# A two-level Winograd matmul with bias and tanh: output stores issued by ScalarE, the first columns of B loaded in wider runs, the first bias load placed later

## The chip, the cores and the metric

The kernel runs on one core of a Trainium2 chip. The core has five engines, each with its own queue of instructions: TensorE (PE in the profile; its weight loads are PEld), VectorE (DVE), ScalarE (ACT), GpSimd (POOL) and SyncE (SP). In this kernel POOL and SP issue all the DMAs. The metric is the device time of one execution in microseconds (us); the median of several runs is compared.

## The reference

```python
m, k, n = 4096, 4096, 4096        # a: [m, k], b: [k, n], bias: [n], all float32
def reference(a, b, bias):
    return np.tanh(np.matmul(a, b) + bias)
```

## The kernel before

**The arithmetic.** A and B are cast to fp16 while they are loaded, products accumulate in fp32 in PSUM (8 banks of 128 x 512), and the output is float32. The output's columns are worked in four groups of 1024 (`c` = 0 to 3); in a group B is cut in four blocks, b11 and b12 (upper half of K, left and right 512 columns), b21 and b22 (lower half of K). The rows of A go in 16 pairs of 128-row tiles, with a11, a12, a21 and a22 likewise. A pair needs seven products in place of eight, by Winograd's scheme: the sums of A's blocks are `s1` to `s4`, those of B's are `t1` to `t4`, and the products are P1 to P7. Many of these products are cut once more by the same scheme: `fine_right` (line 672) makes the sums of a block of B (`f1`, `f2`, `f3`, `f4`), `fine_left` (line 534) those of A (`y`, `z`, `v`), and the seven small products `p1` to `p7` have 256 columns each (`fine_product`, line 702, matmuls at line 709). Whole products have 512 columns (`product`, line 687, matmuls at line 694).

**The start.** The first eight row tiles of A (0 to 7) of the first column group are done without the scheme, straight from `land`ed tiles (lines 1318 to 1496, matmuls at line 1402), so that PE can begin as soon as a few tiles are there. A is loaded in its natural layout and turned: A's first four tiles, `first` (line 1319, four POOL DMAs of 256-byte pieces), by TensorE transposes (`turn_first`, line 1434), all others by VectorE transposes (lines 437 and 1365). PE's order is fixed: `turn_first(0)`, `turn_first(1)`, `row(0)`, `turn_first(2)`, `row(1)`, `turn_first(3)`, `row(2)`, `row(3)` (k tile 0, both halves of 1024 columns), then k tile 1 of the four row tiles, then k tiles 2 and 3, one row tile and one half at a time. Then row tiles 4 to 7 are done over k tiles 0 to 7, and so on. Sums that must leave their bank for a while go to `spill` (ACT copies at line 405) and come back by VectorE (lines 1427 and 402). Where they come back for the last time the bias is added (`take_up` with `k0`), so the first bias is needed there.

**B's loads.** K is laid over the partitions in four quarters of 32 partitions. The usual load of a piece of B (`load_b`, line 604, with its DMAs at line 620) is four POOL DMAs, one for each quarter, each into 32 partitions. `raw_b` loads four k tiles of 512 columns into one buffer (destination runs of 512 fp16 elements). `both_columns` (line 1335) loads two k tiles of all 1024 columns into one buffer (runs of 1024), two buffers to a block. In group 0, the first four k tiles of b11 and b12 are loaded by neither: eight single DMAs (line 615), each one k tile of 512 columns over all 128 partitions; the other three blocks of b11 and b12 come by `raw_b`, and the lower half (b21, b22) by `both_columns`. A DMA of any of these forms moves 128 KB of fp16. A subtraction of blocks (`subtract`, line 632) is cut in as many instructions as the block with the most buffers has buffers.

**Buffers.** SBUF is handed out in 51 `places`; a buffer takes a place when the planner starts its first writer and gives it back when its last user is done. So a load can have to wait until the store of what lay in the place before has landed.

**The order of the work** is written out by a planner (`Plan`, lines 128 to 334). The kernel adds operations with an engine, a duration, reads and writes. `rank` gives each a due time, counted back from those that need it: a DMA's due time is earlier by its issue, by 2 us, by its bytes over a rate, and by 4 us more. With `soft`, an operation is due soon after what it needs. `schedule` then plays the run through: each engine in turn takes the ready operation with the earliest due time, if there is room for its buffers. The order in which they were taken is the order in each engine's queue on the chip, and each queue is worked strictly in order there. A DMA counts as one issue (0.34 us on SP, 0.55 on POOL for each part); its bytes flow in a model with two pipes, one for hardware DMAs (SP) and one for POOL's, which share the bandwidth, and `RING` limits how many may be under way in each (8 and 16).

**Stores.** All 256 output stores (128 x 512 float32, 256 KB) are issued by SP: 112 by `store` (line 413, DMA at line 416), 144 by `finish_in` (line 1045, DMA at line 1050). Each comes after a tanh on ACT that writes its source. SP also issues the bias loads (`load_bias`, line 775), the copies of A's turned tiles and sums to DRAM and back (`move`, line 485, DMA at line 493) and the partial sums `state` (lines 1186 and 1241).

**ACT's work** beside tanh is copies from PSUM to PSUM or SBUF (line 405). In a fine product (`Fine`, line 970) one of them stands between `p1` and `p2`: `p1` is made in bank `be`, ACT copies it to bank `al`, and `p2` is added there. `step` (line 1140) puts the third part of the product before (16 matmuls of 256 columns) between the two on PE.

Of the kernel before, what the change touches and what calls it, by code (L numbers as in the profile page):

```python
# [37 lines left out]
LATER = 6  # L38
PLAIN = (0, 0, 0, 0)
SMALL = 5  # L40
RING = (16, 8)
RISE = ((), (3, 3, 3, 3, 3, 3, 3, 3), (3, 4, 4, 4, 4, 4, 4, 4), (3, 4, 4, 4, 4, 4, 4, 4))
SECONDS = (0, 4, 5, 8)
STEEP = (
# [83 lines left out]
class Plan:  # L128
# [77 lines left out]
    def schedule(self):  # L206
        self.rank()
        places = Places(PLACES)
        queue = {cls: [] for cls in UNITS}
        for i, b in enumerate(self.bufs):  # L210
            if b.users:
                b.order = (b.due, i)
                insort(queue[b.cls], b.order)
        ready = {e: [] for e in ("PE", "DVE", "ACT", "POOL", "SP")}
        busy = dict.fromkeys(ready, 0.0)
        pipes = ([], [])
        clock = [0.0, 0]
        events = [(0.0, -1, 0)]
        for op in self.ops:
            op.left = len(op.preds)  # L220
            op.ready = 0.0
            if not op.left:
                insort(ready[op.eng], (op.due, op.n))
        done, small = 0, [0]
        under_way = dict.fromkeys(ready, 0)

        at_pe = [min(op.due for op in self.ops if op.eng == "PE")]

        def fits(op):
            want = [b for b in op.bufs if b.place is None]  # L230
            near = (at_pe[0] + (op.early or 1e9), 0)
            for b in want:
                until = min(b.order, near)
                e4, e2, e1 = (bisect_left(queue[cls], until) for cls in UNITS)
                w, h, q = places.room()
                same = sum(x.cls == b.cls for x in want) - 1
                q2 = max(0, (e1 - q + 1) // 2)
                if b.cls == "big":
                    e2 = min(e2, max(0, SMALL - small[0]))
                    ok = w > max(same, e4 + max(0, (e2 + q2 - h + 1) // 2))  # L240
                elif b.cls == "out":
                    ok = h + 2 * max(0, w - e4) > max(same, e2 + q2)
                else:
                    ok = q + 2 * max(0, h + 2 * max(0, w - e4) - e2) > max(same, e1)
                if not ok:
                    return False
            return not want or op.due <= at_pe[0] + min(op.reach, self.FAR if op.early else 1e9)

        def flow(now):

            live = [p for p in pipes if p]
            for p in live:
                p[0][0] -= (now - clock[0]) / len(live)
            clock[0] = now
            ended = False
            for p in live:
                while p and p[0][0] < 1e-6:
                    op = p.pop(0)[1]
                    op.done = now + 2.0
                    heapq.heappush(events, (op.done, op.n, 1))  # L260
                    ended = True
            return ended

        def next_flow(now):
            live = [p for p in pipes if p]
            if live:
                clock[1] += 1
                at = now + max(min(p[0][0] for p in live), 1e-6) * len(live)
                heapq.heappush(events, (at, clock[1], 3))

        while events:
            now = events[0][0]
            while events and events[0][0] <= now + 1e-9:
                _, n, kind = heapq.heappop(events)
                if kind == 3 and n == clock[1]:
                    flow(now)
                    next_flow(now)
                elif kind == 4:
                    op = self.ops[n]
                    flow(now)  # L280
                    pipes[op.hw].append([op.lag - 2.0, op])
                    next_flow(now)
                elif kind == 1:
                    op = self.ops[n]
                    done += 1
                    for b in op.bufs:
                        b.users -= 1
                        if not b.users:
                            places.give(b.place)
                            small[0] -= b.cls == "out"  # L290
                    if op.nbytes:
                        under_way[op.eng] -= op.parts
                        for s in op.succs:
                            s.left -= 1
                            if not s.left:
                                heapq.heappush(events, (now, s.n, 2))
                elif kind == 2:
                    op = self.ops[n]
                    insort(ready[op.eng], (op.due, op.n))
            for eng, waiting in ready.items():  # L300
                if busy[eng] > now + 1e-9:
                    continue
                for i, (_, n) in enumerate(waiting):
                    op = self.ops[n]
                    if op.nbytes and under_way[eng] + op.parts > RING[op.hw]:
                        break
                    if not fits(op):
                        continue
                    waiting.pop(i)
                    for b in op.bufs:  # L310
                        if b.place is None:
                            b.place = places.take(UNITS[b.cls])
                            small[0] += b.cls == "out"
                            queue[b.cls].remove(b.order)
                    op.start = now
                    if eng == "PE":
                        at_pe[0] = op.due
                    end = now + op.dur
                    busy[eng] = end
                    heapq.heappush(events, (end, -1, 0))  # L320
                    if op.nbytes:
                        under_way[eng] += op.parts
                        heapq.heappush(events, (end, n, 4))
                        break
                    op.done = end + op.lag
                    heapq.heappush(events, (op.done, n, 1))
                    for s in op.succs:
                        s.ready = max(s.ready, end if s.eng == eng else op.done)
                        s.left -= 1
                        if not s.left:  # L330
                            heapq.heappush(events, (s.ready, s.n, 2))
                    break
        assert done == len(self.ops), (done, len(self.ops))
        return sorted(self.ops, key=lambda op: (op.start, op.n))
# [3 lines left out]
def kernel(  # L338
# [73 lines left out]

    def store(o, row, col, n):
        add(
            "SP", 0.34,
            lambda: nc.sync.dma_start(out=out[ds(row * P, P), ds(col, n)], in_=o[ALL]),
            (o,), (), nbytes=P * n * 4, soft=1.0,
        )

# [181 lines left out]
    def block(name):  # L601
        return Block([new(name, [P, TB, NB], atoms=2 * TB)])

    def load_b(buf, c, k0, nt, j=None, t0=0, early=0.0):

        dx, dt = (1, QP) if k0 >= TB else (TB, 1)
        n, first = (2 * NB, c * NCW) if j is None else (NB, c * NCW + j * NB)
        k1 = k0 - k0 % TB
        off = b.offset + (k1 * QP + (k0 - k1) * dt) * N + first
        one = nt == 1  # L610

        def emit():
            if one:
                src = bass.AP(tensor=b.tensor, offset=off, ap=[[KQ * N, 4], [dx * N, QP], [1, n]])
                nc.gpsimd.dma_start(out=buf[ALL, t0], in_=src)
                return
            for q in Q_ORDER:
                src = bass.AP(tensor=b.tensor, offset=off + q * KQ * N, ap=[[dx * N, QP], [dt * N, nt], [1, n]])
                dst = buf[ds(q * QP, QP)]
                nc.gpsimd.dma_start(out=dst.rearrange("p t j n -> p t (j n)") if j is None else dst, in_=src)  # L620

        add(
            "POOL", 0.55 * (1 if one else 4), emit, (),
            ((buf, (2 * t0, 2 * t0 + 1)) if one else buf,),
            nbytes=nt * P * n * 4, hw=False, early=early, rate=325e3 if j is not None else 362e3,
        )

# [144 lines left out]

    def load_bias(c):
        k = {}
        k["b1"] = new("bias", [P, 2, NB], fp32, atoms=2)
        src = bias[ds(c * NCW, NCW)]
# [3 lines left out]
                out=k["b1"][ALL].rearrange("P a b -> P (a b)"),  # L782
                in_=bass.AP(tensor=src.tensor, offset=src.offset, ap=[[0, P], *src.ap]),
            ),
            (), (k["b1"],), nbytes=P * NCW * 4,
        )
        return k

# [256 lines left out]
    def finish_in(tl, s, row, col):  # L1045

        act(NB, lambda: nc.scalar.activation(tl[ALL, s], tl[ALL, s], TANH), ((tl, (s,)),), ((tl, (s,)),), soft=2.0)
        add(
            "SP", 0.34,
            lambda: nc.sync.dma_start(out=out[ds(row * P, P), ds(col, NB)], in_=tl[ALL, s]),  # L1050
            ((tl, (s,)),), (), nbytes=P * NB * 4, soft=1.0,
        )

# [286 lines left out]
        for i, buf in enumerate(bufs):  # L1340
            load_b(buf, 0, h * T + blk * TB + 2 * i, 2)

    for name in ("b11", "b12"):
        bop[name, 0] = block(name)
    for t in range(TB):
        for j in range(2):
            load_b(bop[f"b1{j + 1}", 0].bufs[0], 0, t, 1, j, t)
    for blk in range(1, 4):
        raw_b(bop, 0, "b11", blk)
        raw_b(bop, 0, "b12", blk)  # L1350
    for blk in H1:
        both_columns(1, blk)

# [118 lines left out]
    for m, j in rows4:  # L1472
        down(4 + m, j, TP - 2, TP, stop=True)
        put_aside(4 + m, j)
        take_up(m, j)
    k0 = load_bias(0)
    for m, j in rows4:
        down(m, j, TB, TP)
    across(g0, TP, T - 2)
# [118 lines left out]
```

## Time and profile before

| What | us |
|---|---|
| median of 3 runs (lowest, highest) | 1507.9 (1506.04, 1508.3) |
| the profiled execution's own time | 1499.22 |
| span of the profiled execution | 1497.2 |
| PE busy in the span | 1460.0 |
| DVE busy | 1170.4 |
| ACT busy | 437.9 |
| POOL busy | 313.9 |
| 16 DMA engines: share of the hardware queue, of POOL's queue | 60.6%, 32.8% |
| mean granted TensorE clock | 0.994 |

Busy time is that of compute instructions and, on POOL, of issuing DMAs; DMA issues on SP and ACT are not counted as busy. In a line of groups "L405" is a line of the kernel, "x8" the number of instructions, and a name such as `ps<-b,o` tells what is written and read, with buffer numbers left out. "Idle before" is the time for which the engine stood before an instruction, with what ended it. Time to landing runs from the issue of a DMA until its completion mark is full. All times in a trace count from the start of its span.

### The profile page before, as it was taken

The page shows a single profiled execution, that of the slowest core. Times are in us where ns is not written, and L with a number is a line of the kernel's source. Part 1 is how long each engine was busy: PE and PEld are TensorE (multiplying, and loading weights), DVE is VectorE, ACT ScalarE, POOL GpSimd, SP SyncE. Part 2 cuts the span into 40 slices and gives each one's busy share as a digit, 9 for nine tenths or more (in the row PEclk, how much of TensorE's full clock was granted, in tenths as well). Part 3 has the DMA queues.
Part 4 walks back from the last instruction along what each step waited for, and adds up shares of the span by engine and source line. Part 5 has one row for each costly group of instructions (what it writes and reads, how often), then busy time and mean ns, then how long its engine had stood idle before and what let it go on. Part 6 is the DMA issues. An engine that isn't in the chain of part 4 may idle for free.

```text
span 1497.2 us, 28113 instructions
## 1 busy us (share of the span) xinstructions
PE 1460.0 (98%) x10811; PEld 1058.9 (71%) x10811; DVE 1170.4 (78%) x1816; ACT 437.9 (29%) x986; POOL 313.9 (21%) x581
## 2 busy tenths in 40 slices
PE   7999999999999999999999999999899899999998
PEld 3444445554568666666778868888788788888887
DVE  1767997778688878888688969887678678887675
ACT  1211111211123222433333322244333333234433
POOL 7764334334523101110220300000112210000000
PEclk8999999999999999999999999999999999999999
DMA  9999899899999999999999989688989998778773
GB/s 157 167 222 223 208 243 234 222 218 221 261 281 290 291 333 312 329 353 347 277 301 367 312 290 303 211 279 277 260 251 317 278 247 281 240 234 273 255 254 111
DMA packets 213014, 394.06 MB, mean 263 GB/s; under 512 B 30480, under 2 KB 93968, under 8 KB 212880
## 3 DMA queue, kind: packets, MB, share of 16 engines
q1 hardware_dynamic: 126864, 316.73, 60.6%
q0 software_dynamic: 86016, 75.55, 32.8%
q8 instruction: 84, 1.38, 0.4%
q14 instruction: 50, 0.41, 0.1%
HBM read 321.39 MB, written 146.28 MB: 312 GB/s over the span
## 4 chain that ended last, share of the span: by engine, by line
PE 83%; DMA 10%; DVE 4%; POOL 1%; issue 1%; ACT 1%; SPq 0%; DVEq 0%; ACTq 0%; POOLq 0%
PE ps L709 54%; PE ps L694 25%; PE ps L1402 4%; DMA nat<-in_a_dram 2%; DMA out_dram<-st 2%; DMA b<-in_b_dram 1%; DMA a<-a 1%; DMA xa<-a 1%; DVE a L437 1%; DMA out_dram<-cs 1%; DMA out_dram<-parts 1%; DVE o L437 0%; DVE s L402 0%; DMA land<-in_a_dram 0%; POOL b L620 0%
## 5 line engine op out<-in xcount | busy, mean ns | idle before, releaser
L620 POOL DMA_DIRECT2D b<-in_b_dram x248 | 133.7, 545 | 562.5 <-DVE ps L402 210.7
L451 POOL DMA_DIRECT2D nat<-in_a_dram x256 | 137.2, 542 | 326.0 <-DMA s<-s 102.1
L694 PEld LDWEIGHTS <-s 128*128 128x128 f16 x1056 | 103.0, 98 | 120.2 <-DVE s L402 5.0
L405 ACT COPY ps<-ps 128x256 f32<-128x256 f32 (+1 forms) x255 | 93.4, 366 | 322.6 <-PE ps L709 310.3
L694 PEld LDWEIGHTS <-a 128*128 128x128 f16 x928 | 91.0, 98 | 108.7 <-DVE a L402 3.9
L437 DVE STREAM_TRANSPOSE a<-nat 128x256 f16<-128x256 f16 (+2 forms) x192 | 154.8, 857 | 15.0 <-PE ps L694 8.7
L694 PE MATMUL ps<-b,a 128*128 128x512 f16 x672 | 151.9, 381 | 3.4 <-DVE a L402 3.4
L709 PEld LDWEIGHTS <-a 128*128 128x128 f16 x1320 | 129.1, 98 | 27.4 <-issue 3.4
L709 PEld LDWEIGHTS <-zs 128*128 128x128 f16 x1248 | 122.1, 98 | 16.1
L694 PE MATMUL ps<-t,s 128*128 128x512 f16 x576 | 129.4, 379 | 2.8 <-DVE s L402 2.8
L709 PEld LDWEIGHTS <-ys 128*128 128x128 f16 x1248 | 122.1, 98 | 14.1
L1402 PE MATMUL ps<-b,o 128*128 128x512 f16 x512 | 115.6, 387 | 9.1 <-DMA b<-in_b_dram 7.8
L709 PEld LDWEIGHTS <-ya 128*128 128x128 f16 x1120 | 109.6, 98 | 16.1 <-DVE ya L402 2.9
L709 PEld LDWEIGHTS <-za 128*128 128x128 f16 x1120 | 110.0, 98 | 14.6 <-issue 0.8
L405 ACT COPY parts<-ps 128x256 f32<-128x256 f32 (+1 forms) x165 | 64.4, 391 | 179.0 <-PE ps L709 86.9
L694 PE MATMUL ps<-b,s 128*128 128x512 f16 x480 | 111.1, 379 | 0.7 <-DVE s L402 0.7
L402 DVE TENSOR_TENSOR parts<-ps,parts 128x256 f32<-128x256 f32 (+1 forms) x155 | 68.5, 442 | 42.3 <-PE ps L709 28.6
L1402 PEld LDWEIGHTS <-o 128*128 128x128 f16 x512 | 50.3, 99 | 72.4 <-issue 11.8
L423 ACT ACTIVATE parts<-ps 128x512 f32<-128x512 f32 x66 | 39.4, 597 | 201.5 <-PE ps L694 111.9
L402 DVE TENSOR_TENSOR ps<-ps,parts 128x256 f32<-128x256 f32 (+1 forms) x170 | 75.8, 448 | 28.8 <-PE ps L709 20.2
L709 PE MATMUL ps<-b,a 128*128 128x256 f16 x656 | 85.0, 273 | 1.5 <-ACT ps L405 1.5
L709 PEld LDWEIGHTS <-xs 128*128 128x128 f16 x736 | 72.0, 98 | 15.3 <-issue 6.3
(118 smaller groups left out, 2468.1 us busy)
## 6 DMA issues: line engine op xcount, KB each, us to landing
a<-a SPq DMA_DIRECT2D x75, 512.0 KB, 6.5
a<-a SPq DMA_DIRECT2D x150, 256.0 KB, 6.4
b<-in_b_dram POOLq DMA_DIRECT2D x256, 128.0 KB, 8.0
nat<-in_a_dram POOLq DMA_DIRECT2D x256, 128.0 KB, 7.1
out_dram<-parts SPq DMA_DIRECT2D x112, 256.0 KB, 5.6
ys<-s SPq DMA_DIRECT2D x46, 512.0 KB, 5.0
xs<-s SPq DMA_DIRECT2D x46, 512.0 KB, 4.8
s<-s SPq DMA_DIRECT2D x38, 512.0 KB, 5.6
```

The lines of the kernel that those rows point to most:

```text
L402: dve(n, lambda: nc.vector.tensor_tensor(out=o(), in0=x(), in1=y(), op=op), reads, writes, wide, **kw)
L405: act(n, lambda: nc.scalar.copy(o(), x()), reads, writes, **kw)
L423: act(NB, lambda: nc.scalar.activation(o[ALL], src[ALL], TANH), (src,), (o,), soft=2.0)
L437: nc.vector.transpose(dst[:, ds(t, n), :].rearrange("P t (mb p) -> P mb t p", p=QP), src[:, :, ds(t * QP, n * QP)].rearrange(order, x=QP),)
L451: nc.gpsimd.dma_start(out=tl[(ds(q * QP, QP), *key)], in_=src)
L620: nc.gpsimd.dma_start(out=dst.rearrange("p t j n -> p t (j n)") if j is None else dst, in_=src)
L694: nc.tensor.matmul(bank[ALL], left[ALL, k + t, ALL], rb.tile(t), start=start and k == t0 and t == 0, stop=k + t == t0 + nt - 1, skip_group ...
L709: nc.tensor.matmul(bank[ALL, HALF[half]], buf[ALL, at_ * TP + i * TB + t, ALL], rb.tile(t), start=False, stop=i == 1 and t == TB - 1, skip ...
L1402: nc.tensor.matmul(bank[ALL], left[ALL, t, ALL], rb.tile(tb), start=start, stop=stop, skip_group_check=True,)
```

## The change

It has three parts.

1. Both store functions issue on ACT's queue (`nc.scalar.dma_start`) and not on SP's. The planner counts the 0.34 us on ACT, has a third pipe for ACT's DMAs, and a limit of 8 under way for it.
2. The first four blocks of b11 and b12 of group 0 are loaded by `both_columns`, as the lower half is: 32 DMAs of 32 partitions, two k tiles by 1024 columns each, take the place of eight single-tile DMAs and 24 DMAs of four k tiles by 512 columns. The single-tile form of `load_b` is gone.
3. The load of the first bias may not start before the last PE operation that was added ahead of it (`after=plan.last_pe`): the last step of row tiles 4 to 7 over k tiles 0 to 7.

```diff
-RING = (16, 8)
+RING = {"POOL": 16, "SP": 8, "ACT": 8}
...
-        pipes = ([], [])
+        pipes = {e: [] for e in RING}
...
-                    pipes[op.hw].append([op.lag - 2.0, op])
+                    pipes[op.eng].append([op.lag - 2.0, op])
...
-                    if op.nbytes and under_way[eng] + op.parts > RING[op.hw]:
+                    if op.nbytes and under_way[eng] + op.parts > RING[eng]:
...
     def store(o, row, col, n):
         add(
-            "SP", 0.34,
-            lambda: nc.sync.dma_start(out=out[ds(row * P, P), ds(col, n)], in_=o[ALL]),
+            "ACT", 0.34,
+            lambda: nc.scalar.dma_start(out=out[ds(row * P, P), ds(col, n)], in_=o[ALL]),
             (o,), (), nbytes=P * n * 4, soft=1.0,
         )
...
-            if one:
-                src = bass.AP(tensor=b.tensor, offset=off, ap=[[KQ * N, 4], [dx * N, QP], [1, n]])
-                nc.gpsimd.dma_start(out=buf[ALL, t0], in_=src)
-                return
...
-            (), (k["b1"],), nbytes=P * NCW * 4,
+            (), (k["b1"],), nbytes=P * NCW * 4, after=after,
...
-            "SP", 0.34,
-            lambda: nc.sync.dma_start(out=out[ds(row * P, P), ds(col, NB)], in_=tl[ALL, s]),
+            "ACT", 0.34,
+            lambda: nc.scalar.dma_start(out=out[ds(row * P, P), ds(col, NB)], in_=tl[ALL, s]),
...
-    for name in ("b11", "b12"):
-        bop[name, 0] = block(name)
-    for t in range(TB):
-        for j in range(2):
-            load_b(bop[f"b1{j + 1}", 0].bufs[0], 0, t, 1, j, t)
-    for blk in range(1, 4):
-        raw_b(bop, 0, "b11", blk)
-        raw_b(bop, 0, "b12", blk)
+    for blk in range(4):
+        both_columns(0, blk)
...
-    k0 = load_bias(0)
+    k0 = load_bias(0, plan.last_pe)
```

More of the change, by code (lines that the diff above doesn't have):

```diff
@@ L249, in flow @@
         def flow(now):
-            live = [p for p in pipes if p]
+            live = [p for p in pipes.values() if p]
             for p in live:
@@ L264, in next_flow @@
         def next_flow(now):
-            live = [p for p in pipes if p]
+            live = [p for p in pipes.values() if p]
             if live:
@@ L602, in block, with load_b @@
         return Block([new(name, [P, TB, NB], atoms=2 * TB)])
-    def load_b(buf, c, k0, nt, j=None, t0=0, early=0.0):
+    def load_b(buf, c, k0, nt, j=None, early=0.0):
         dx, dt = (1, QP) if k0 >= TB else (TB, 1)
@@ L609, in load_b @@
         off = b.offset + (k1 * QP + (k0 - k1) * dt) * N + first
-        one = nt == 1
         def emit():
-            if one:
-                src = bass.AP(tensor=b.tensor, offset=off, ap=[[KQ * N, 4], [dx * N, QP], [1, n]])
-                nc.gpsimd.dma_start(out=buf[ALL, t0], in_=src)
-                return
             for q in Q_ORDER:
@@ L622, in load_b @@
         add(
-            "POOL", 0.55 * (1 if one else 4), emit, (),
-            ((buf, (2 * t0, 2 * t0 + 1)) if one else buf,),
+            "POOL", 4 * 0.55, emit, (), (buf,),
             nbytes=nt * P * n * 4, hw=False, early=early, rate=325e3 if j is not None else 362e3,
@@ L771, in fine, with load_bias @@
             return sb
-    def load_bias(c):
+    def load_bias(c, after=None):
         k = {}
```

## The prediction

> **What bounds the kernel now.** I read the page's busy table first, then busy time by stretch, then what TensorE waited for, then the order of events at the start. The busy table:
>
> ```profile
> span 1497.2 us, 28113 instructions
> PE 1460.0 (98%) x10811; PEld 1058.9 (71%) x10811; DVE 1170.4 (78%) x1816; ACT 437.9 (29%) x986; POOL 313.9 (21%) x581
> ```
>
> TensorE (PE) is busy for 98% of the span. Its 10811 matmuls are untouched by the change, so only the 37 us in which it stands, and its slow clock, can move. Busy time by stretch shows where:
>
> ```profile
> 0.00:12.00 12.00, 6.42 (x26) 2.85 (x27) 0.93 (x4) 1.93 (x3) 9.26 (x18) 0.86 0.92 129
> 12.00:24.00 12.00, 8.36 (x31) 3.25 (x29) 2.98 (x6) 2.89 (x6) 7.94 (x15) 0.78 1.26 159
> 24.00:48.00 24.00, 23.85 (x107) 10.30 (x104) 12.79 (x19) 6.33 (x12) 16.76 (x30) 0.96 1.26 169
> 75.00:125.00 50.00, 49.72 (x231) 22.39 (x230) 36.21 (x43) 7.87 (x14) 30.03 (x57) 1.00 1.11 224
> 153.00:200.00 47.00, 43.55 (x224) 21.94 (x223) 43.52 (x60) 8.84 (x17) 17.38 (x33) 0.96 0.91 205
> ```
>
> The columns are PE, PEld, DVE, ACT, POOL, granted clock, DMA share, GB/s. PE stands 5.6 + 3.6 us in the first 24 us, at a clock of 0.86 and 0.78. From 153 to 200 VectorE (DVE) is nearly full. What PE waited for, the longest in total:
>
> ```profile
> PE ps L709 <- DVE ps L402: 10.3, 7, 3.8
> PE ps L1402 <- DMA b<-in_b_dram: 7.8, 5, 4.1
> ...
> PE ps L709 <- ACT ps L405: 2.0, 3, 1.3
> ```
>
> B's first tiles cost 7.8 us in five waits, and ScalarE (ACT) holds PE up for only 2.0 us in the whole run. PE's order of events at the start (start, length, idle before):
>
> ```profile
> 10.68 1.01 PE L1402 MATMUL ps<-b,o 128*128 128x512 f16 x2 [4.12 <-DMA b<-in_b_dram]
> 16.36 2.10 PE L1402 MATMUL ps<-b,o 128*128 128x512 f16 x9 [1.26 <-DMA b<-in_b_dram]
> 18.71 0.38 PE L1402 MATMUL ps<-b,o 128*128 128x512 f16 x1 [0.24 <-DMA b<-in_b_dram]
> 20.55 0.38 PE L1402 MATMUL ps<-b,o 128*128 128x512 f16 x1 [1.46 <-DMA b<-in_b_dram]
> 21.59 4.65 PE L1402 MATMUL ps<-b,o 128*128 128x512 f16 x13 [0.67 <-DMA b<-in_b_dram]
> ```
>
> From 21.59 on PE runs nearly without a hole to 122, so what the start loses is lost for good.
>
> **B's first block.** Removed: eight DMAs of line 615 (128 rows by 512 columns each). Added: eight of the form of line 620 (32 rows, two k tiles by 1024 columns), which B's lower half has today. All move the same 128 KB. The query of line 615 says:
>
> ```profile
> L615 POOL DMA_DIRECT2D b<-in_b_dram x8: 671/685/725, 3.7 to 13.5; - x8
> ...
> DMA to landing us min/median/max: 5.7/6.7/8.1
> ```
>
> The landings in the trace tell more. The first 17 POOL DMAs end from 5.39 to 22.19: 16 steps in 16.8 us, 1.05 us a step, and the slow steps are the eight of line 615. The next eleven end by 29.47: 0.66 us a step. Those of line 620 with 1024 columns, ending from 77.17 to 92.36, also take 0.66 us. The very first tile DMA has 12 of its 16 landing marks by 7.35 and the last four from 10.02 to 10.54, so it rides on few DMA engines while the others stand.
>
> After: the planner's due time falls with a transfer's size, so I expect the first 1 MB of B (four DMAs) ahead of the four loads of A's first tiles. The first DMA ends at 5.39 as now, three more at 0.66 make 7.4, two loads of A at about 0.9 (they step 0.71 and 1.06) make 9.2, the transposes 0.6: first product at 9.8 and not 10.68. That saves 0.9. It brings both of the first two k tiles. A's other two loads end at 11.0, B's second half at 13.6, or at 16.3 if the four loads of `land` go ahead of it. PE needs 4.4 us for the first eight products with their transposes (10.68 to 15.1 now) and 1.7 to 3.4 for the next eight: it is done at 15.9 to 17.6. So the four later waits, measured between matmul starts at 1.68, 0.41, 1.62 and 0.83, sum 4.5, go but for some 0.2. Together **5.2 us**. The granted clock is 0.50 from 22.4 to 25.8, behind the stretch with the holes. If the holes go, up to 1.7 us of work is saved; I take 0.8, the middle. Start: **-6.0**, bounds -2 (if A's loads go first and PE waits later for A) and -7.
>
> What is late next: POOL's row of DMAs, which feeds the `land` transposes at 47 to 50 (PE stands 1.4 us there). It runs some 5 us earlier too, since the slow steps are gone from it.
>
> **Blocks 1 to 3 and the wider tiles.** Step 0.66 before and after: nothing. With two buffers to a block, `t1` is made in eight subtractions instead of four, and the fine right side of b11 in 16 instead of 8. A 128x2048 one takes 1.215 us, a 128x1024 one 0.684: a split costs 0.15, so 12 splits cost 1.8 us of DVE. The first 0.6 lie at 77 to 82, where PE is covered; 1.2 lie in 153 to 200, where DVE is on the chain. Bounds 0 and 1.8; I take half of the 1.2: **+0.6**.
>
> **Bias.** Its 512 KB leave the first 4 us and come after about 47 us. It is needed at 59.8 and landed in 3.6: hidden. The DMA work that it puts ahead of POOL's loads is 512 KB at 200 to 300 GB/s, 1.7 to 2.6 us; loads wait for free places there (POOL's waits on PE and DVE), so I take **0**. Without that cover it costs 2.2.
>
> **The stores.** 256 stores leave SyncE's queue (SP), 102 us of issue there in the trace's records, 0.40 us each.
>
> ```profile
> L1050 SPq DMA_DIRECT2D out_dram<-st x48: 332/338/1600, 562.6 to 1489.7; - x48
> ...
> DMA to landing us min/median/max: 2.0/5.3/13.9
> ```
>
> On ACT each blocks what stands behind it: about 0.06 for the tanh in front to finish and 0.40 to issue. Behind it stand the copies that PE needs. The tightest is the copy after `p1`: PE then runs 16 products of 256 columns (0.109 each, 1.75 us) before `p2` needs it, and the copy takes 0.36 + 0.08, so 1.3 us are spare. Today two tanh in a row (2 x 0.63) stand ahead of copies, and PE still waits only 2.0 us. Two stores add 0.92 to the 1.26: 2.0 x 0.92/1.26 = **+1.5**. Bounds 0 and 13 (below). SP's loads no longer stand behind stores that wait for a tanh, but the same bytes go through the same DMA engines (share 0.8 to 1.1 in most stretches). PE's holes from 423 to 1166, 16 us in all, lie where a load waits for a place that a store frees; they can shrink or grow with the new order by some 6 us: **0**.
>
> The Trainium skill, "DMA: Bandwidth & Descriptors", section "Issuing engines are not separate DMA queues", says that issuing from several engines saves only the sequencer's time. By it SP's relief moves no byte sooner; the sum stays as it is, since I took 0 for it.
>
> **Sum.** -6.0 + 0.6 + 1.5 = -3.9. The profiled execution took 1499.2 us (span 1497.2 and 2.0 around it): 1495.3. The runs shown have a median of 1507.9, 8.7 more than the profiled one; with that difference kept, **1504.0**. Some 3 us, 0.2%, is what a measurement of this kernel can tell from no change, so the forecast is a small gain.
>
> **Rivals.**
> - *The gain is given back.* DMA rows of 104 to 112 us: POOL's queue holds 51% of the engines and 0.68 MB beside SP's 62%, where it had 118% and 1.59 MB at 88 to 96. If stores and loads on two hardware queues each press POOL's, its third part of some 300 GB/s is 100 instead of 150. In 20 us of overlap that is 1 MB, 5 us of POOL's steps, of which I put 3 on the path: **1507**. Against it: stores and loads share one byte count in either case. The skill's page named above, section "Queues, rings and completion order", gives such turns by packet between queue rows; no run here shows three live at once. Chance 0.19.
> - *ACT stands in the way* (slower). If the copy after `p1` lies behind two tanh and two stores, 2.18 us, it is 0.9 us late. 192 stores lie in columns 1 to 3, 96 pairs. Eight late pairs beyond those in the 1.5 cost 7 us, from where it is slower. Ten, in place of the 1.5, make **1511**, fifteen (13 us) 1516. For it: ACT is busiest there, 9.7 of 25 us. Against it: the planner counts 0.34 for a store and places the copy first. Chance 0.25.
> - *The start does not move* (the change doesn't do what it says): PE waits for A in place of B. Then 0.6 + 1.5 remain, and bias's 2.2: **1512**. Chance 0.10.
>
> **Chances.** Forecast 0.46 (its own range 1498 to 1505), faster; given back 0.19, within 0.2%; the two others 0.35, slower. The range takes in the bounds of the start and of the holes, and the slower cases to fifteen pairs: 1497 to 1516.
>
> **What would show it.** First product near 10 and no waits for B to 22; the half clock at 22 gone; PE's products up to 120 us some 5 us earlier. PE's wait on ACT copies: 3 to 4 us by the forecast, over 9 by the second rival. POOL's DMA steps in 100 to 200 us still 0.66 when alone. I am wrong if the first product comes after 11, or if new holes over 6 us come from the new order of SP's loads.

## The result and the profile after

| | before | after |
|---|---|---|
| median of the runs (lowest, highest), us | 1505.3 (1500.91, 1508.3), 6 runs | 1524.7 (1518.19, 1526.44), 6 runs |
| ratio of after to before, 95% interval | 1 | 1.012 [1.0093, 1.0147] |
| span of the profiled execution, us | 1497.2 | 1523.8 |
| PE's holes in that execution, us | 35.0 | 58.1 |
| mean granted clock | 0.994 | 0.992 |

The kernel became 1.2% slower, some 19 us by the medians. The forecast was 1504.0, a small gain, and its range ended at 1516. "Holes" here and below are the times between the starts of two matmuls beyond what the first one takes at full rate, where they are over 0.25 us, summed over one profiled execution.

The busy table of after:

```profile
span 1523.8 us, 28090 instructions
PE 1465.6 (96%) x10811; PEld 1060.4 (70%) x10811; DVE 1170.5 (77%) x1828; ACT 442.0 (29%) x986; POOL 311.8 (20%) x581
```

The work is the same: PE's 10811 matmuls, and 12 more VectorE instructions, the wider tiles' splits. The span grew by 26.6 us: PE stands 21.0 us more (37.2 before, 58.2 after; 23.1 by the count of holes), and its busy time grew by 5.6 us. The clock has a part in the latter: behind 400 us it was 0.50 for 17.1 us in after and for 3.4 us in before. The stretches of the start (PE, PEld, DVE, ACT, POOL, granted clock, DMA share, GB/s):

```profile
0.00:12.00 12.00, 6.97 (x27) 3.07 (x28) 1.16 (x6) 1.93 (x3) 9.98 (x21) 0.84 1.04 159
12.00:24.00 12.00, 12.00 (x53) 5.35 (x52) 5.24 (x10) 4.66 (x10) 10.48 (x20) 0.87 1.28 196
24.00:48.00 24.00, 23.11 (x106) 10.00 (x105) 11.74 (x16) 4.01 (x8) 15.29 (x28) 1.00 1.14 157
75.00:125.00 50.00, 50.00 (x234) 22.65 (x232) 32.98 (x43) 8.43 (x15) 29.33 (x55) 1.00 1.10 212
153.00:200.00 47.00, 42.85 (x226) 21.80 (x225) 43.92 (x68) 10.03 (x19) 17.16 (x32) 1.00 0.89 210
```

The start is better, as forecast: PE has no hole from 12 to 24, and the clock is 0.87 and then 1.00, where it was 0.78 and 0.96. PE's order of events there (start, length, idle before):

```profile
9.12 1.33 PE L1428 MATMUL tp<-ident,first 128*128 128x128 f16 x8 [3.52 <-DMA first<-in_a_dram]
10.24 1.06 PE L1390 MATMUL ps<-b,o 128*128 128x512 f16 x2
...
12.80 18.52 PE L1390 MATMUL ps<-b,o 128*128 128x512 f16 x80
```

The first product starts at 10.24 and not at 10.68, and from 12.80 on 80 matmuls run with no wait for B. What PE waited for in the whole run (total, times, longest):

```profile
PE ps L703 <- DVE ps L402: 25.2, 19, 3.8
PE ps L703 <- ACT ps L405: 7.8, 5, 4.0
PE ps L703 <- DVE ya L402: 4.3, 1, 4.3
...
PE tp L1428 <- DMA first<-in_a_dram: 3.5, 1, 3.5
```

B's 7.8 us are gone. The wait on VectorE's additions in PSUM rose from 10.3 to 25.2, the wait on ScalarE's copies from 2.0 to 7.8.

Where the loss lies is seen when both traces are laid side by side at the same amount of matmul work done. At before's 21.6 us, after is 4.5 us ahead; at 50, 6.1; at 200 and at 400, 4.2. Then it loses: 1.4 behind at 520, 10.1 at 700, 18.0 at 850, 22.3 at 1200, 26.4 at the end. So part 2's gain is in the trace, and 30 us are lost after 400, where B's first columns are long done and stores leave all the time.

One hole from there, followed back. PE, then DVE, both of after:

```profile
586.14 1.03 PE L703 MATMUL ps<-t,zs 128*128 128x256 f16 x8 [2.75 <-DVE ps L402]
```

```profile
582.00 0.69 DVE L402 TENSOR_TENSOR ys<-a 128x1024 f16<-128x1024 f16 x1 [1.47 <-DMA out_dram<-cs]
...
585.69 0.40 DVE L402 TENSOR_TENSOR ps<-ps,edge 128x256 f32<-128x256 f32 x1
```

PE stands 2.75 us until DVE's addition at 585.69. DVE had stood 1.47 us until 582.00, since `ys` was to be written into a place from which a store of `cs` was still being read. ACT issued that store at 574.83 and it landed 7.1 us later; the planner had put 5.6 us. The addition that PE needed stood behind `ys` in DVE's queue, and DVE worked without a break in between, so the store's late landing accounts for 1.47 of the 2.75 us. Behind 400 us, PE's waits of over 0.3 us sum to 36.6 us in after and to 14.2 in before; in 33.3 and 6.8 us of them the engine that PE waited for had itself stood for a store within the 14 us before. That is a count of what came first, not a proof for each wait. The trace's view of the stores says how often such a thing happens (line, queue, issues; who waited for a store, us, times; time to landing):

```profile
L416 ACTq DMA_DIRECT2D out_dram<-parts x112: 338/338/375, 95.3 to 1273.0; - x112
...
  ACT parts L423: 40.7, 12
  ACT parts L405: 21.0, 7
  DVE zs L402: 19.5, 7
  DVE t L402: 15.9, 4
  DVE za L402: 15.0, 4
...
DMA to landing us min/median/max: 2.0/5.5/10.8
```

The stores take as long to land as before (median 5.41 us before, 5.49 after), but ACT and DVE stand for them 159.2 us in sum, where it was 80.5. (POOL's waits for stores fell, from 23.5 to 16.3.)

### The profile page after: what moved, and what is told of

Read it like the earlier page. It is cut to its first block, busy times and chain, and to the rows that moved or that the text cites. A ratio compares the mean times of both kernels' runs of the same rounds, so it can differ in the third digit from the quotient of the medians.

```text
span 1523.8 us, 28090 instructions
## 1 busy us (share of the span) xinstructions
PE 1465.6 (96%) x10811; PEld 1060.4 (70%) x10811; DVE 1170.5 (77%) x1828; ACT 442.0 (29%) x986; POOL 311.8 (20%) x581
## 4 chain that ended last, share of the span: by engine, by line
PE 74%; DMA 14%; DVE 7%; issue 2%; POOL 2%; ACT 1%; ACTq 0%; SPq 0%; DVEq 0%; POOLq 0%
PE ps L703 46%; PE ps L688 23%; PE ps L1390 4%; DMA a<-a 3%; DMA out_dram<-p 3%; DVE a L437 2%; DMA s<-a 2%; DMA out_dram<-parts 1%; DMA out_dram<-cs 1%; POOL b L615 1%; DMA out_dram<-st 1%; DMA land<-in_a_dram 1%; DVE s L402 1%; DMA nat<-in_a_dram 1%; DVE a L402 1%
## 5 line engine op out<-in xcount | busy, mean ns | idle before, releaser
L615 POOL DMA_DIRECT2D b<-in_b_dram x256 | 137.6, 543 | 591.4 <-DMA s<-s 209.9
L437 DVE STREAM_TRANSPOSE a<-nat 128x256 f16<-128x256 f16 (+2 forms) x192 | 155.2, 858 | 8.2 <-PE ps L703 3.0
```

Of the source, the lines that this page charges most:

```text
L437: nc.vector.transpose(dst[:, ds(t, n), :].rearrange("P t (mb p) -> P mb t p", p=QP), src[:, :, ds(t * QP, n * QP)].rearrange(order, x=QP),)
```

## The experiments

Three theories stood after the result. **The plan:** with a third pipe the planner believes that stores land sooner than they do, so it writes work that reuses their places too early into in-order queues. **The queue:** an issue on ACT delays what stands behind it. **The count:** 8 + 8 under way in place of 8 press the loads. The rival that a new order scatters the time by itself was there too, and later a rival within the plan, called "shares": that the third pipe makes the planner time the loads wrongly, and not the stores.

What the planner believes can be read from its own clock as it plays the run through. All 256 stores, issue to landing, median: planned 4.29 us before and 3.81 after. A pipe's turn is its share of the bandwidth, so a store in SP's pipe queues behind loads, and a store in a pipe of its own gets a third at once. I compare each store with the trace in the order of issue: 16% landed over 2 us later than planned before, 36% after.

**Each part alone.** e1 is before with part 2's `both_columns` only; e2 is before with part 1 only.

```diff
# e1
...
+    for blk in range(4):
+        both_columns(0, blk)
# e2
+RING = {"POOL": 16, "SP": 8, "ACT": 8}
...
+        pipes = {e: [] for e in RING}
...
+            "ACT", 0.34,
+            lambda: nc.scalar.dma_start(...)
...
```

> Part 2 alone: B's first columns by wide runs, stores still issued by SP, bias early. If the start was predicted rightly (first product near 10.2 us, no waits for B until 30 us, PE some 5 us earlier at 120 us) and the loss comes from the stores alone (theory 'ACT's queue'), this is 3 to 6 us faster than before: ratio 0.996 to 0.998. If any new order of the planner costs as much as the change did (theory 'new order': the start moves every later operation in the planner's clock), new stalls beyond 400 us eat it: ratio 1.000 or more.

> Part 1 alone: stores planned for and issued by ACT, with a third pipe; B and bias as before. Theory 'ACT's queue' (a store that must wait holds up the copies behind it on ACT): slower by what the change lost plus what its start gained, ratio 1.012 to 1.018, with several stores of ACT standing over 0.6 us before their issue and holes in PE beside them. Theory 'new order': could land anywhere from 0.995 to 1.02, and the holes lie where SP's loads come late, not beside waiting stores.

e1: 0.9981 [0.9963, 1.0]; e2: 1.014 [1.0109, 1.0171]. The loss is part 1's. e1 is 4.6 us ahead at 200 and at 800 us and 1.1 at the end, so most of the start's gain is lost after 800 us, by an order that is new too.

**The order and the queue apart.** e3 keeps after's order and issues the stores on SP; e4 keeps before's order and issues them on ACT; e8 is e4 with POOL.

```diff
# both store functions
# e3, on after           # e4, on before           # e8, on before
-nc.scalar.dma_start     -nc.sync.dma_start        -nc.sync.dma_start
+nc.sync.dma_start       +nc.scalar.dma_start      +nc.gpsimd.dma_start
```

> The changed kernel with the planner's order exactly as it is there (stores planned on ACT), but each store issued by SP at its place in that order. Theory 'ACT's queue': with the stores off ACT the time falls to 0.995 to 1.000 of before. Theory 'new order': the order is what costs, so it stays at 1.008 to 1.015.

> The kernel before with the planner's order exactly as before (stores planned on SP), but each store issued by ACT at its place in that order. Theory 'ACT's queue': slower, ratio 1.008 to 1.02. Theory 'new order': 0.998 to 1.004, since the order of all else is that of before.

> The kernel before, its order kept, but each store issued by POOL (software queue with completion semaphores of its own), which is mostly idle beyond 430 us. ACT is left alone here. If the 0.76% that the same order lost with stores on ACT came from stores holding ACT (waiting for a semaphore that a load of SP holds), this is 0.997 to 1.003. If it came from SP's loads no longer being held behind stores, or from a third stream of DMAs, it is 1.005 to 1.012 here too. POOL's own loads may be held by a store before 430 us, which could add up to 0.003.

e3: 1.0185 [1.0151, 1.0218]; e4: 1.0076 [1.005, 1.0102]. With the stores off ACT, after's order costs even more than the whole change, though its stores then stand in a queue that it was not written for; the queue alone costs 0.8% in an order that was written for SP. e8: 1.0216 [1.0186, 1.0246], above both of its forecasts; it tells nothing apart, since on POOL the stores also stand ahead of its own loads.

**The pipe or the count.** On after: e5 lets SP and ACT together have 8 under way, e6 puts ACT's stores in SP's pipe, e7 does both, e11 is e6's order with the stores issued by SP.

```diff
# e5, e7
+HW = ("SP", "ACT")
-if op.nbytes and under_way[eng] + op.parts > RING[eng]:
+if op.nbytes and sum(under_way[e] for e in (HW if eng in HW else (eng,))) + op.parts > RING[eng]:
# e6, e7, e11
-pipes[op.eng].append([op.lag - 2.0, op])
+pipes["SP" if op.eng == "ACT" else op.eng].append([op.lag - 2.0, op])
```

> The changed kernel, but the planner lets SP and ACT together have 8 hardware DMAs under way (the chip's waits show eight completion semaphores that both queues take in turn), not 8 each. If the loss in the order comes from the planner counting on 16 under way, this falls from 1.012 to about 1.004 of before (what stays is ACT's hold, some 1.0076 less the start's gain of 0.002 to 0.004). If the count is not the point, it stays at 1.010 to 1.015.

> The changed kernel, but the planner sends SP's and ACT's bytes through one pipe, as before, while the count stays at 8 each. If the loss in the order comes from the third pipe (a store in a pipe of its own is planned to take a third of the bandwidth at once, so loads are planned at other times than they land), this falls to about 1.004. If not, 1.010 to 1.015.

> The changed kernel with one pipe and one count of 8 for SP and ACT together: the planner sees one hardware queue again and differs from before in what a store costs (0.34 us of ACT and not of SP) and in B's loads. If the model of the queues explains the part of the order, about 1.004, the size of ACT's hold less the start's gain. If any replanning with stores on ACT costs, 1.010 or more.

> The version with one pipe (1.000), its order kept, each store issued by SP. In that version 13 stores stand 0.8 to 4.1 us on ACT for a semaphore (29 us in sum). If those holds cost, SP issue is faster here: 0.994 to 0.998. If they are covered and SP's order, planned without the stores in it, suffers from having them, 1.004 to 1.015, as with the changed kernel's own order (1.0185 against 1.012).

e5: 1.0108 [1.0073, 1.0143]: the count is not the cause. e6: 0.9999 [0.9977, 1.002], e7: 1.0003 [0.9986, 1.002]: with one pipe the loss is gone, although ACT still issues the stores. e11: 0.9938 [0.9918, 0.9957]: in this order ACT's issue costs 0.6%.

**The dose.** The third pipe stays, and only the landing that the planner adds to a store's flow (2 us) is changed: e13 to 3, e9 to 4, e14 to 6; e15 is e9's order issued by SP. e10 goes the other way: e6's single pipe, which had no loss, with 0.

```diff
# e9; e13 has 3.0, e14 6.0, e10 0.0
-op.done = now + 2.0
+op.done = now + (4.0 if op.eng == "ACT" else 2.0)
```

> The changed kernel with the planner's stores landing 1 us later (planned mean 5.1; the trace has 5.4). If the loss follows the error of the planned landing, this lies between 1.012 (mean 4.1) and 0.9936 (6.0): 1.000 to 1.006. If 2 us merely drew a lucky order, anything from 0.994 to 1.015.

> The changed kernel, third pipe kept, but the planner lets each store land 2 us later (its planned median from issue to landing goes from 3.8 to 5.7 us, mean 4.1 to 6.0; the trace of the changed kernel has 5.5 and 5.4). Theory 'stores planned to land too early' (places are counted free before they are, and what takes them stands in its queue): falls from 1.012 to 0.998 to 1.004. Theory 'shares' (the third pipe plans SP's and POOL's loads too slow, p90 of POOL 23.9 against 22.7 with one pipe): stays at 1.009 to 1.015, since the loads' plan is as in the changed kernel.

> The changed kernel with the planner's stores landing 4 us later (planned mean 8.1, p90 9.3; the trace has 5.4 and 8.0). With the error gone on the other side: 0.992 to 0.998, a little lost at most to places counted as taken longer than they are. If 2 us was a lucky order, anything up to 1.01.

> The order of the 2 us version (0.9936), each store issued by SP. If ACT's issue costs what it cost in the other two orders that were planned soundly (0.6 to 0.8%), this is 0.986 to 0.990. If stores that a sound plan puts on ACT cost nothing there, 0.993 to 1.000.

> The version with one pipe for SP and ACT (1.000), but the planner lets each store land 2 us earlier (planned mean 6.0 to 4.0, median 2.2, as optimistic as the changed kernel's). Theory 'stores planned to land too early': rises to 1.006 to 1.015. Theory 'shares': stays at 0.998 to 1.003.

e13: 1.0008 [0.9992, 1.0025]; e9: 0.9936 [0.9914, 0.9958]; e14: 0.9914 [0.9884, 0.9944]; e15: 0.9918 [0.9891, 0.9946]; e10: 1.0294 [1.0257, 1.033]. One constant of the planner takes the loss away, and the opposite change brings more than it back. Both went further than was expected (0.998 to 1.004 for e9, 1.006 to 1.015 for e10). Both speak against "shares": e9 keeps the third pipe and has no loss, e10 has none and loses. PE's waits in e9, and then in e10:

```profile
PE ps L703 <- DVE ps L402: 11.5, 8, 3.3
...
PE ps L703 <- ACT ps L405: 2.5, 3, 1.1
```

```profile
PE ps L703 <- ACT ps L405: 23.5, 12, 5.6
PE ps L703 <- DVE ps L402: 19.5, 16, 3.0
```

The line that rose to 25.2 in after is at 11.5 in e9, near before's 10.3, with the stores still on ACT and three queues live. In e10 ACT itself stands for stores (135 us, against 76 in after), and PE for ACT.

**Before's own margin.** If a late landing is what costs, before itself, with 16% of its stores over 2 us late, should gain from a longer one. e18 is before with 4 us for its stores, e16 is e1 with 4, e17 is e1 with 6. e12 only plans an issue at 0.40 us in place of 0.34, to see what a new order does by itself.

```diff
# e16, e18; e17 has 6.0
-op.done = now + 2.0
+op.done = now + (4.0 if op.soft == 1.0 and op.eng == "SP" else 2.0)
# e12, in both store functions
-            "SP", 0.34,
+            "SP", 0.40,
```

> The kernel before, with a store's issue planned at 0.40 us and not 0.34 (nearer to the trace's mean of 0.40): a small change of the planner's clock that leaves queue and pipes alone, to see how much a new order by itself moves the time. If orders scatter by chance as much as the change did, anything from 0.99 to 1.012. If the change's loss has a cause of its own, this stays within 0.997 to 1.003.

> B's wide runs alone, stores planned on and issued by SP (0.998), with the planner's stores landing 2 us later (planned mean 5.5 to 7.3, measured 5.4). The order before was already planned with the right mean, so by the landing theory little is left to gain: 0.994 to 0.999. If later planned landings always help, whatever the queue: 0.988 to 0.993.

> B's wide runs, stores on SP, planned to land 4 us later: the candidate for the best. If the margin goes on paying, 0.984 to 0.990; if 2 us took what there was (0.9902), 0.988 to 0.994.

> The kernel before with nothing changed but the planner's stores landing 2 us later. If the margin is a lever by itself, 0.990 to 0.995 (e16's 0.9902 less the wide runs' 0.002). If it only repairs orders that the wide runs or ACT had spoilt, 0.998 to 1.002.

e12: 1.0013 [0.999, 1.0037]; e18: 0.9928 [0.9902, 0.9954]; e16: 0.9902 [0.9877, 0.9927], 1489.0 us, the fastest of all; e17: 0.9921 [0.9902, 0.994]. So a later landing gains 0.7 to 0.8% where nothing had been lost, too, and e9's step from 1.012 to 0.9936 is more than the repair. Nearest to the repair by itself is e13: planned at 5.07 us in the mean, near before's 5.45, it takes before's time. Together, sorted by what the planner believed (the stores' median landing as planned; measured; the share over 2 us late; ACT's and DVE's waits for a store's landing and PE's holes in the profiled execution):

| kernel | issued by | planned us | landed us | over 2 us late | waits us | PE's holes us | ratio |
|---|---|---|---|---|---|---|---|
| e10 | ACT | 2.20 | 5.22 | 48% | 198.5 | 73.5 | 1.0294 |
| after | ACT | 3.81 | 5.49 | 36% | 159.2 | 58.1 | 1.012 |
| e6 | ACT | 4.20 | 5.48 | 20% | 91.6 | 36.3 | 0.9999 |
| before | SP | 4.29 | 5.41 | 16% | 80.5 | 35.0 | 1 |
| e1 | SP | 4.34 | 5.32 | 16% | 84.9 | 34.1 | 0.9981 |
| e13 | ACT | 4.74 | 5.32 | 12% | 92.7 | 39.2 | 1.0008 |
| e9 | ACT | 5.74 | 5.48 | 5% | 68.4 | 31.0 | 0.9936 |
| e16 | SP | 6.01 | 5.45 | 4% | 28.5 | 29.0 | 0.9902 |
| e18 | SP | 6.02 | 5.25 | 3% | 23.6 | 27.9 | 0.9928 |
| e14 | ACT | 7.74 | 5.61 | 0% | 15.4 | 29.7 | 0.9914 |
| e17 | SP | 8.10 | 5.31 | 1% | 2.9 | 27.7 | 0.9921 |

The stores land in 5.2 to 5.6 us whatever is planned, and the time follows the share that is late, within some 0.3%. The four others whose stores leave from the engine that was planned fit too: e2 (32% late, 1.014), e5 (35%, 1.0108), e7 (20%, 1.0003), e12 (15%, 1.0013). Those whose stores leave from another engine than was planned do not: e3 (31%, 1.0185), e4 (17%, 1.0076), e8 (17%, 1.0216), e11 (18%, 0.9938), e15 (11%, 0.9918). There the queue counts as well. From about 5.7 us planned, at or above what is measured, nothing more is to be won: e17 has next to no waits left, and its time is no better than e16's or e18's.

## Why the prediction was wrong, point by point

- **Start, -6.0: right up to 70 us, in part by luck.** Forecast: first product near 10 (9.8), no waits for B, the half clock gone. Measured: 10.24, none, clock 1.00 from 24 to 48, and a lead of 6.1 us at 50 us. PE's first wait is now for A (3.5 us). B's second half landed at 13.85 (13.6 or 16.3 forecast), at 0.65 us a step; in the first half the steps were 0.67, 0.64 and 1.19 us. The lead was 4.5 us at 21.6, where 5.2 were forecast; the other 1.6 came where before ran at the clock of 0.50 from 22.4 to 25.8, priced at 0.8. That the holes make this half clock is not shown: e18 has before's loads and waits 6.9 us for B, and its clock is 1.00 there. What is late next was named but priced at nothing, and it came at another place. DVE, in after:

```profile
70.21 1.29 DVE L402 TENSOR_TENSOR t<-b 128x1024 f16<-128x1024 f16 x2 [0.21 <-PE ps L1390]
71.42 2.31 DVE L437 STREAM_TRANSPOSE o<-land 128x2048 f16<-128x2048 f16 x1
```

  Two `t` subtractions stand ahead of the last `land` transpose, where before has them behind it (at 77.02). PE stands 2.8 us for that transpose (a new hole at 73.78, which the trace puts down to `DVE o L437`), and 3.4 us of the lead are left at 100.
- **The wider tiles, +0.6: not settled.** The lead goes from 3.8 to 4.2 across 153 to 200, but that is no proof that the splits cost nothing: before ran at a clock of 0.50 for 3.4 us from 196.4, which after did not, and after has a wait of 0.53 us for DVE at 185.19 that before has not. e1, with the same splits, does not have that wait.
- **Bias, 0: right in size, wrong in what happens.** I let the load move behind 47 us. In after's trace SP still issues it at 0.81 us:

```profile
0.81 0.39 SPq L775 DMA_DIRECT2D bias<-in_bias_dram  x1
```

  The condition binds the planner only. On the chip nothing waits for that PE operation, and the load is still first in SP's queue. So part 3 did not move the load on the chip. No run takes part 3 alone.
- **The stores' issue on ACT, +1.5: mis-sized.** It is 0.8% in e4 (11 us) and 0.6% between e6 and e11 (9 us), near the upper bound of 13; between e9 and e15 it is 0.2%, which the intervals do not tell from nothing; and in after's own order it is the other way about, since e3, with SP issuing, is 0.6% slower than after. So it has no one size. What I left out is a hold. In after's ACT order:

```profile
642.12 0.63 ACT L1041 ACTIVATE cs<-cs 128x512 f32<-128x512 f32 x1
645.10 0.34 ACTq L1044 DMA_DIRECT2D out_dram<-cs  x1
```

  The tanh is done at 642.75, and the store leaves 2.35 us later, because ACT waits for a completion semaphore. The DMAs of SP and ACT take eight of these in turn, so a store on ACT waits for the DMA that had its semaphore before, mostly one of SP's copies of A's tiles and sums (here `s<-ys`, which landed 0.08 us before the store left). In after 16 stores are held so for over 0.2 us, 25.6 us in sum. PE feels it: four of its five waits for ACT's copies, 6.7 of the 7.8 us, come right behind a held store. The longest, ACT and then PE:

```profile
1178.40 0.34 ACTq L1044 DMA_DIRECT2D out_dram<-p  x1
1178.78 0.38 ACT L405 COPY ps<-bias 128x256 f32<-128x256 f32 x1 [4.69 <-DMA a<-a]
```

```profile
1179.48 1.87 PE L703 MATMUL ps<-b,xa 128*128 128x256 f16 x8 [3.97 <-ACT ps L405]
```

  But this is not the 1.2%: e6 has 16 such stores, with 30.3 us, and is no slower than before. How the cost splits between hold and issue in e4, e6 and e9 stays open.
- **The order of SP's loads and the places that stores free, "they can shrink or grow with the new order by some 6 us: 0": the step that failed.** PE's holes grew by 23 us, where the prediction had named new holes of over 6 us as a sign that it is wrong. I looked at the diff's third pipe and asked what it does to the DMAs; I did not ask what it does to the plan. In the median it moved no store sooner (5.41 and 5.49 us to land; the slowest tenth took over 9.4 us before and over 8.0 after), but it made the planner free the stores' places 0.5 us earlier in the median and 1.35 in the mean (5.45 planned before, 4.10 after), so that ACT and DVE stand for 79 us more. What stood for the places was these two engines' writes; the prediction had loads in mind. The Trainium skill, "DMA: Bandwidth & Descriptors", section "Issuing engines are not separate DMA queues", has it that the engine which issues does not change the DMA engines that carry the bytes; the two medians agree. The planner with its third pipe had the median fall from 4.29 to 3.81, which no trace here bears out.
- **The rivals.** "ACT stands in the way" had the right sign, and its mark (ACT copies over 9 us) was nearly reached at 7.8, by holds for a semaphore and not by the issues that it counted; against 25.2 for DVE's additions it is the smaller part. "The gain is given back" by three live queues: e9 has the same three and gains 0.6%. "The start does not move" is refuted by the lead of 6.1 us, though PE's first wait did pass from B to A.

**Open:** how much of a single order's 0.1 to 0.4% is scatter (e12 moves by 0.1%, inside its interval; e6 and after differ in more than the stores' landing), and why e11 gains 0.6% with as many late stores as before has. The 3.5 us that e1 loses after 800 us are in the main of the same kind: at 1078 its DVE stands 8.81 us for a store of `cs` (6.24 at the same place in before), PE 5.79 (3.22), and the clock behind it is 0.50 for 6.8 us.

## What to carry to other kernels

When an order is written out by a model, a change to the model's queues is a change to every in-order queue of the kernel: compare what the model believes of each transfer, issue to landing, with the trace, and do so first. Plan a landing at or above the measured time: too early makes an in-order engine stand with all that is behind it, too late by some 2 us cost nothing that could be measured here. And a dependency that only the planner knows is no wait on the chip.

## What the runs showed of the hardware that was not expected

- A store of 256 KB under this load lands in 5.2 to 5.7 us in the median, on SP's queue or ACT's.
- In these programs SP's and ACT's DMAs share eight completion semaphores, taken in turn (POOL's have eight others); a store on ACT was held up to 4.3 us by one (at 1178 us in after). Whether another share-out would end the holds, no run shows.
- The first single-tile load of B in before (128 rows in one DMA) had 12 of its 16 landing marks by 7.35 us and the last four at 10.02 to 10.54. The first 17 POOL DMAs of before, eight of them such loads, stepped 1.05 us on average; loads of the same 128 KB over 32 partitions each step 0.66. The Trainium skill, "DMA: Bandwidth & Descriptors", section "Why a DMA increments its semaphore by 16 and not by 1", says that a DMA rides on as many engines, up to 16, as divide the slowest dimension of both sides; the source's was 4 there and is 32 now. The four late marks agree.
- The granted clock was 0.50 from 22.4 to 25.8 us in before and 1.00 there in after, but also 1.00 there in e18, which keeps holes at the start; so what sets it stays open. From 400 to 520 us, where after's new holes begin, it is 0.97, where it was 1.00.
